# A hybrid RWKV-7 / forgetting-attention layer on one core: all engines' instruction order made with the scheduler's finer timing model

## The chip, the cores and the metric

The kernel runs on one core of one Trainium2 chip. The time is that of the whole launch on the device in microseconds (us). Of several runs the median is taken.

## What is computed

One layer of a streaming encoder is computed for two inputs: 1024 new frames of a prompt (no past) and 64 frames of a running stream (256 cached frames). Cut to what matters:

```python
h    = rms_norm(x, norm1_g) * (1 + sc1) + sh1              # sc, sh, gt: silu(c) @ w_ada + b_ada
proj = h @ w_in                                            # 1792 RWKV columns, 1544 attention columns
z    = p_rwkv + (previous_row(p_rwkv) - p_rwkv) * shift_mu # -> r, k, v, decay, a, g
...
def step(s, inp):                                          # RWKV-7, one frame after the other, 8 heads of 64
    sa = einsum('bhvk,bhk->bhv', s, -kk_t)
    s  = s * w_t + sa * (kk_t * a_t) + v_t * k_t
    return s, einsum('bhvk,bhk->bhv', s, r_t)
...
y_fox = softmax(q k^T / 8 + decay_bias, causal) @ v        # 8 heads of 64, q and k RMS-normed
x = x + gt1 * (concat(y_rwkv, y_fox) @ w_out)
h2 = rms_norm(x, norm2_g) * (1 + sc2) + sh2
x = x + gt2 * ((silu(h2 @ w_ffn_gate) * (h2 @ w_ffn_up)) @ w_ffn_down)
```

Also returned are the last RWKV state and row, and the attention keys, values and log forget values.

## The kernel before

All matrices stand transposed, features on the 128 partitions and frames along the free axis. The frames are cut into two halves: half 0 has prompt frames 0 to 511, half 1 has prompt frames 512 to 1023 and the 64 stream frames (576 columns, handled as two chunks of 288). Every large product is made to near single precision by three matmuls on split operands (`mm3`, L294 to L296: high times high, high times low, low times high, all into one PSUM tile).

The stages, in the order in which the program is written:

- Modulation (L190, L198) and the normed input of half 0.
- For each half a phase (`phase`) that runs a handwritten list of small tasks, `ORDER`: Z are the input projections of one pair of RWKV heads (PSUM tile `pmm`), Q, K, V those of attention, D, A, B and N the RWKV work of one pair of heads, T and U the B and N left over from the half before. There are 4 pairs (j = 0 to 3) in each half, so 8 RWKV chains in all.
- Attention of half 0, attention of half 1 with the output projection of half 0 between its heads, the output projection of half 1.
- The FFN (L1153) in 44 passes of 7 products, and the down projection (L1264).

**One RWKV chain.** The recurrence is done in chunks of 64 frames. A (`rwkv_a`) makes the scaled operands and the chunk matrices (TensorE L464 into `pA`, VectorE L466 into `At`), sends 16x16 blocks through DRAM, solves them with 15 pairs of small VectorE operations (L488, L490) and sends the result back through DRAM. B (`rwkv_b`) joins the blocks with 32x32 matmuls (L523, L549; `pg`, `pw`, `pu`, `pgt`), transposes (`pkbt`, `pvt`), and then walks through the chunks, 8 in half 0 and 9 in half 1, one strictly after the other. One **step** of this walk is:

```python
nc.tensor.matmul(pr, At[:, c, 0], sv[:, c], ...)                    # L597, pR
nc.vector.tensor_copy(R[hsl[0]], pr[hsl[0], 0])                     # L599
nc.scalar.copy(R[hsl[1]], pr[hsl[1], 1])                            # L600
nc.tensor.matmul(py[:, c % 4], sv[:, c], rk[:, c], ...)             # L608, pY
nc.tensor.matmul(pa, inv[:, c], R, ...)                             # L610, pSA
nc.vector.tensor_scalar(sv[hsl[0], c, 0], pa[hsl[0]], -1.0, ...)    # L611
nc.scalar.mul(sv[hsl[1], c, 1], pa[hsl[1]], -1.0)                   # L612
nc.tensor.matmul(pS, kbt[:, c], sv[:, c], ...)                      # L613, pS
nc.vector.scalar_tensor_tensor(d, pS[hsl[h], h], pc[...], sd[...])  # L617, twice; next chunk's sv
nc.tensor.matmul(py[:, c % 4], sv[:, c], At[:, c, 1], ...)          # L618, pY
```

So a step has three **links** in which TensorE needs a result that other engines make of its own last one: pR to pSA (through L599 and L600), pSA to pS (through L611 and L612), pS to the next pR (through L617). GpSimd scales the old state meanwhile (L604, `sd`). The ninth chunk starts from another state, so the link ahead of it is none. N (`rwkv_n`) then normalizes (`bsum`, L375; ScalarE L637, L639; `plora`, L368).

**What sets the order.** The program is written through a tile framework. It records every instruction with its dependences, and when its context closes, a scheduler decides for each of the five engines in which order its instructions stand; tasks written earlier have precedence, and a task that would have to wait lets later ones pass. To judge what would have to wait, the scheduler runs a timing model as it goes. On the chip each engine then takes its instructions in that fixed order, with semaphores between engines. SyncE (SP) issues all DMAs, in its own fixed order. PSUM for the attention of half 1 is only opened when the pools of the RWKV phase are closed. The context is opened in `kernel`:

## Time and profile before

| | |
|---|---|
| median of 3 runs | 1747.09 us (1741.33 to 1749.53) |
| the profiled execution | 1735.94 us |
| its span, first to last instruction | 1734.2 us |
| TensorE matmul busy (PE) | 1663.8 us, 96% |
| TensorE weight load busy (PEld) | 1447.9 us, 83% |
| VectorE busy (DVE) | 1126.6 us, 65% |
| ScalarE busy (ACT) | 729.1 us, 42% |
| GpSimd busy (POOL) | 180.8 us, 10% |

The profile is of one execution. PE and PEld are two rows of one engine: the matmuls, and the loading of the matrices that stay in the array, which runs beside them. PE's ends of matmuls are modelled, so that PE busy is not PE at its peak. A float32 matmul of the program shows as two records. "L597 pR" is line 597 writing tile pR; an arrow in brackets names who ended the idle time before.

### The profile page before, as it was taken

The numbers are of one execution on the slowest core, as the hardware profiler recorded it, in microseconds if no ns is written. First come the engines' busy times: TensorE is split into PE (matmuls) and PEld (weight loads), VectorE is DVE, ScalarE is ACT, GpSimd is POOL, SyncE is SP. The second block draws the span as 40 slices with busy tenths as digits, with TensorE's granted clock in tenths as the row PEclk, the third lists the DMA queues.
The fourth block names the chain that finished last, engine by engine and source line by source line (L and its number), as shares of the span: only waits on it lengthen the run. The fifth ranks groups of instructions, "written<-read, shape, count | busy, mean of one in ns | idle before, by whom it ended". The sixth has DMA issues, their size and how long they took to land.

```text
span 1734.2 us, 33257 instructions
## 1 busy us (share of the span) xinstructions
PE 1663.8 (96%) x12893; PEld 1447.9 (83%) x12893; DVE 1126.6 (65%) x2574; ACT 729.1 (42%) x1532; POOL 180.8 (10%) x412
## 2 busy tenths in 40 slices
PE   5999999999999999889999989999999999999999
PEld 3676766688888888766888889999999999999998
DVE  6676676757686753876877686666666655555545
ACT  4534454553454445765776453333233223211210
POOL 2102121131221212300210000000000000000000
PEclk9999999999899999989999999999999999999999
DMA  8535457632233344566553333222222224433213
GB/s 314 149 95 137 142 140 207 175 93 56 55 76 75 95 121 136 157 194 177 151 177 136 127 115 101 75 75 75 76 75 82 78 87 143 161 98 98 95 37 122
DMA packets 133581, 207.09 MB, mean 119 GB/s; under 512 B 62126, under 2 KB 70350, under 8 KB 133422
## 3 DMA queue, kind: packets, MB, share of 16 engines
q1 hardware_dynamic: 133422, 204.95, 39.3%
q8 instruction: 102, 1.67, 0.4%
q14 instruction: 57, 0.47, 0.1%
HBM read 157.65 MB, written 47.25 MB: 118 GB/s over the span
## 4 chain that ended last, share of the span: by engine, by line
PE 82%; DVE 7%; ACT 7%; DMA 2%; issue 2%; SPq 1%; POOL 0%; DVEq 0%; ACTq 0%; POOLq 0%
PE pd L1264 15%; PE pfc L1153 8%; PE pfe L1153 8%; PE pfa L1153 7%; PE pmm L294 5%; PE pmm L296 5%; PE pmm L295 5%; PE pfb L1153 4%; PE pav L962 2%; PE pbs L375 2%; PE pA L464 2%; PE ppt L940 2%; PE po L294 1%; PE po L295 1%; PE po L296 1%
## 5 line engine op out<-in xcount | busy, mean ns | idle before, releaser
L294 PE MATMUL pmm<-hhi,whi 128*128 128x288 f32 (+1 forms) x624 | 220.7, 354 | 0.7 <-ACT pb L317 0.7
L295 PE MATMUL pmm<-hlo,whi 128*128 128x288 f32 (+1 forms) x624 | 218.2, 350 | 0.0
L296 PE MATMUL pmm<-hhi,wlo 128*128 128x288 f32 (+1 forms) x624 | 218.0, 349 | 0.0
L212 ACT CAST whi<-wraw 128x1024 fp32r<-128x1024 f32 (+2 forms) x116 | 99.3, 856 | 214.4 <-PE pd L1264 167.0
L1264 PE MATMUL pd<-ah,wlo 128*128 128x512 f32 (+1 forms) x528 | 173.5, 329 | 0.0
L1264 PE MATMUL pd<-al,whi 128*128 128x512 f32 (+1 forms) x528 | 173.2, 328 | 0.0
L1264 PE MATMUL pd<-ah,whi 128*128 128x512 f32 (+1 forms) x528 | 173.0, 328 | 0.0
L1268 DVE SCALAR_TENSOR_TENSOR x1t<-pd,mod,x1t 128x512 f32<-128x512 f32 x192 | 91.4, 498 | 110.6 <-PE pd L1264 110.0
L294 PEld LDWEIGHTS pmm<-hhi,whi 128*128 128x128 f32 x624 | 120.3, 193 | 13.5 <-ACT pb L317 2.0
L296 PEld LDWEIGHTS pmm<-hhi,wlo 128*128 128x128 f32 x624 | 120.3, 193 | 10.9 <-issue 1.7
L295 PEld LDWEIGHTS pmm<-hlo,whi 128*128 128x128 f32 x624 | 120.4, 193 | 9.6 <-issue 0.7
L216 DVE TENSOR_TENSOR wlo<-wraw,whi 128x1024 fp32r<-128x1024 f32 (+2 forms) x108 | 103.8, 961 | 26.0 <-ACT whi L212 25.6
L1153 PE MATMUL pfc<-hh,hS 128*128 128x256 f32 (+1 forms) x352 | 102.0, 290 | 4.4 <-ACT hh L1055 4.4
L1264 PEld LDWEIGHTS pd<-al,whi 128*128 128x128 f32 x528 | 99.4, 188 | 7.7
L1264 PEld LDWEIGHTS pd<-ah,whi 128*128 128x128 f32 x528 | 99.3, 188 | 7.7
L1264 PEld LDWEIGHTS pd<-ah,wlo 128*128 128x128 f32 x528 | 99.2, 188 | 7.4
L1153 PE MATMUL pfc<-hl,hS 128*128 128x256 f32 (+1 forms) x352 | 102.3, 290 | 0.0
L1153 PE MATMUL pfc<-hh,lS 128*128 128x256 f32 (+1 forms) x352 | 102.0, 290 | 0.0
L1153 PE MATMUL pfa<-hl,whi 128*128 128x256 f32 (+1 forms) x352 | 101.8, 289 | 0.0
L1153 PE MATMUL pfa<-hh,whi 128*128 128x256 f32 (+1 forms) x352 | 101.7, 289 | 0.0
L1153 PE MATMUL pfa<-hh,wlo 128*128 128x256 f32 (+1 forms) x352 | 101.4, 289 | 0.0
L604 POOL TENSOR_SCALAR sd<-sv,pc 64x64 f32<-64x64 f32 x136 | 72.0, 529 | 172.9 <-DVE sv L617 156.6
(360 smaller groups left out, 4402.0 us busy)
## 6 DMA issues: line engine op xcount, KB each, us to landing
wraw<-in_w_in_dram SPq DMA_DIRECT2D x52, 512.0 KB
wada<-in_w_ada_dram SPq DMA_DIRECT2D x48, 512.0 KB
as<-actscr SPq DMA_DIRECT2D x22, 544.0 KB
wraw<-in_w_gate_dram SPq DMA_DIRECT2D x22, 512.0 KB
wraw<-in_w_up_dram SPq DMA_DIRECT2D x22, 512.0 KB
wraw<-in_w_down_dram SPq DMA_DIRECT2D x40, 256.0 KB
wraw<-in_w_out_dram SPq DMA_DIRECT2D x16, 512.0 KB
actscr<-sg SPq DMA_DIRECT2D x22, 288.0 KB
```

The lines of the kernel that those rows point to most:

```text
L212: nc.scalar.copy(hi, src)
L216: eng.tensor_tensor(lo, src, hi.bitcast(F32), op=ALU.subtract)
L294: nc.tensor.matmul(ps[0:M, 0:n], whi[:, k, 0:M], xhi[:, k, off:off + n], start=(k == 0), stop=False)
L295: nc.tensor.matmul(ps[0:M, 0:n], whi[:, k, 0:M], xlo[:, k, off:off + n], start=False, stop=False)
L296: nc.tensor.matmul(ps[0:M, 0:n], wlo[:, k, 0:M], xhi[:, k, off:off + n], start=False, stop=(k == kt - 1))
L375: nc.tensor.matmul(ps[:, 0:n], w, x[:, off:off + n], start=True, stop=True)
L464: nc.tensor.matmul(pa[h][:, i], kb[hp, c + i], rk[hp, c + i], start=True, stop=True)
L604: nc.gpsimd.tensor_scalar(sd[hsl[h]], sv[hsl[h], c, h], pc[hsl[h], c], None, op0=ALU.mult)
L940: nc.tensor.transpose(pt[0:rows, b - b0, t * P:t * P + qn], p[0:qn, pc:pc + rows], self.ident[0:qn, 0:qn])
L1153: nc.tensor.matmul(ps, l[:, k], r[:, s, k], start=(first and k == 0 and y == 0), stop=(k == 3 and y == 2), skip_group_check=True)
L1264: nc.tensor.matmul(ps[:, 0:n], w[:, i], x[:, t:t + n], start=(i == 0 and y == 0), stop=(i == len(fs) - 1 and y == 2))
L1268: nc.vector.scalar_tensor_tensor(dst, ps[:, so - off:so - off + l], self.mod[:, 40 + o, b:b + 1], dst, op0=ALU.mult, op1=ALU.add)
```

## The change

One argument of the tile context. The instructions, their operands, the pools and the number of buffers remain; the scheduler judges what would have to wait with a finer timing model.

```diff
-    with _tile.TileContext(nc) as tc:
+    with _tile.TileContext(nc, schedule_with_timeline_sim=True) as tc:
```

The order changes on every engine from the start to the FFN; in the down projection it hardly does. Two places on TensorE:

First, the walk of the last of the eight chains (half 1, j = 3; `At_7017` is its chunk matrix), from the eighth of its nine chunks. psc, ppt and pav are products of the attention of half 0. Before:

```order
L597 MATMUL pR_8375<-sv_8213,At_7017 128x128
L608 MATMUL pY_8329<-rk_6998,sv_8213 128x128
L940 MATMUL ppt_8963<-ident_130,p_8893 128x128
L940 MATMUL ppt_8963<-ident_130,p_8904 128x128
L940 MATMUL ppt_8972<-ident_130,p_8893 128x128
L940 MATMUL ppt_8972<-ident_130,p_8904 128x128 x2
L962 MATMUL pav_8984<-ptl_8910,vsx0_8029 128x256
L610 MATMUL pSA_8385<-R_8377,inv1_693 128x64
L962 MATMUL pav_8984<-pth_8909,vsx0_8029 128x256
L962 MATMUL pav_8984<-ptl_8910,vsx0_8029 128x256
L910 MATMUL psc_8992<-k1x1_8032,qsx1_8030 128x512
L912 MATMUL psc_8992<-k2x1_8033,q2x1_8031 128x512
```

The same step with the change, up to the group norm (pbs) that closes the chain:

```order
L597 MATMUL pR_8375<-sv_8213,At_7017 128x128
L608 MATMUL pY_8329<-rk_6998,sv_8213 128x128
L610 MATMUL pSA_8385<-R_8377,inv1_693 128x64
L613 MATMUL pS_8383<-sv_8213,kb_6999 128x128
L618 MATMUL pY_8329<-At_7017,sv_8213 128x128
L597 MATMUL pR_8400<-sv_8213,At_7017 128x128
L610 MATMUL pSA_8411<-R_8402,inv1_693 128x64
L608 MATMUL pY_8409<-rk_6998,sv_8213 128x128
L613 MATMUL pS_8408<-sv_8213,kb_6999 128x128
L618 MATMUL pY_8409<-At_7017,sv_8213 128x128
L375 MATMUL pbs_8613<-y_8242,bmean_635 128x288
L375 MATMUL pbs_8616<-y_8242,bmean_635 128x288
```

The attention products that stood in each link have moved ahead of the walk, and the step's own five matmuls now follow each other.

Second, the place where the last input projection ends (`pmm_8549`, the last V projection; pkv and pkvs are its transposes). Before, it ends inside the walk of the last chain (`sv_8213`):

```order
L294 MATMUL pmm_8549<-hhi_175,whi_8519 128x288
L295 MATMUL pmm_8549<-hlo_176,whi_8519 128x288
L296 MATMUL pmm_8549<-hhi_175,wlo_8520 128x288
L814 MATMUL pkv_8575<-ident_130,fv_8516 128x128 x2
L910 MATMUL psc_8673<-k1x0_8027,qsx0_8025 128x256
L912 MATMUL psc_8673<-k2x0_8028,q2x0_8026 128x256
L916 LDWEIGHTS identb_8663
L916 MATMUL psc_8673<-cmask_8670,identb_8663 128x128
L613 MATMUL pS_8253<-sv_8213,kb_6999 128x128
L618 MATMUL pY_8254<-At_7017,sv_8213 128x128
```

With the change it ends inside the walk of the first chain of half 1 (`At_4747`, `sv_5446`), and the joining of the second chain (`At_5686`) follows:

```order
L295 MATMUL pmm_8549<-hlo_176,whi_8519 128x288
L296 MATMUL pmm_8549<-hhi_175,wlo_8520 128x288
L814 MATMUL pkv_8575<-ident_130,fv_8516 128x128 x2
L613 MATMUL pS_5641<-sv_5446,kb_4729 128x128
L618 MATMUL pY_5642<-At_4747,sv_5446 128x128
L523 MATMUL pg1_6339<-gt_696,At_5686 32x32 x18
L814 MATMUL pkv_8575<-ident_130,fv_8516 128x128 x2
L820 MATMUL pkvs_8583<-ident_130,fv_8516 64x128
L523 MATMUL pw1_6379<-g1_6337,inv1_693 32x32 x9
L523 MATMUL pu1_6401<-inv1_693,g1_6337 32x32 x13
L375 MATMUL pbs_6069<-y_5475,bmean_635 128x288
```

The projections have moved forward against the RWKV chains by nearly three chains: ahead of the last `pmm` row stand 60 of the 68 pR rows before, 41 with the change. Of the 8 groups of pA (L464) none stands behind the last `pmm` row before, two do with the change.

Counted over all eight walks, 192 links lie between one step's matmul and the next that needs its result. In 2 of them no matmul of other work stands before; with the change in 97: by chain 7, 9, 9 and 20 in half 0 and 1, 24, 3 and 24 in half 1. In the links that still hold other work there is more of it than before: in the first walk of half 1 it is 3 to 10 matmuls a link before, and with the change mostly 20 to 29.

## The prediction

> **What bounds the kernel now.** I read the page first, for who is busy and when. The rows are the span, TensorE's two shares and, in 40 slices, the clock that it was granted, in tenths.
>
> ```profile
> span 1734.2 us, 33257 instructions
> PE 1663.8 (96%) x12893; PEld 1447.9 (83%) x12893; DVE 1126.6 (65%) x2574; ACT 729.1 (42%) x1532; POOL 180.8 (10%) x412
> PEclk9999999999899999989999999999999999999999
> ```
>
> TensorE is the bound, and the change takes no work from it, so only waits can come or go. Second I read busy times by stage: the start, the RWKV phases, attention to the end of the output projection, and part of the FFN. Columns are PE, PEld, DVE, ACT, POOL (busy us and count), clock, DMA share and GB/s.
>
> ```profile
> 0.00:40.00 40.00, 22.36 (x287) 13.72 (x288) 25.88 (x73) 18.36 (x38) 8.35 (x36) 0.91 0.87 326
> 40.00:720.00 680.00, 656.16 (x5703) 519.20 (x5702) 460.33 (x1253) 329.86 (x757) 140.64 (x306) 0.98 0.43 118
> 720.00:1040.00 320.00, 294.40 (x1918) 247.21 (x1918) 245.01 (x504) 203.02 (x430) 31.78 (x70) 0.96 0.52 154
> 1040.00:1480.00 440.00, 440.00 (x3478) 438.90 (x3478) 263.38 (x500) 135.63 (x249) 0.00 (x0) 1.00 0.28 91
> ```
>
> From 1040 us on TensorE is full, and no order can gain there. What the change can do it does in the first 1040 us. In the RWKV phases PE lacks only 680 - 656 = 24 us. Third I asked who waits there, and read one step of the recurrence, instruction by instruction. First the waits (total us, times, longest):
>
> ```profile
> PEld pS L613 <- ACT sv L612: 16.2, 47, 1.0
> PEld pSA L610 <- ACT R L600: 12.0, 41, 0.8
> PE pada L190 <- DMA wada<-in_w_ada_dram: 11.5, 2, 11.1
> PE pS L613 <- ACT sv L612: 3.1, 7, 0.8
> PE pSA L610 <- ACT R L600: 0.6, 2, 0.3
> ```
>
> Then the step, in order of time (start, duration, engine, what):
>
> ```profile
> 160.16 0.43 PE L610 MATMUL pSA<-R,inv 128*128 128x64 f32 x2
> 160.40 0.48 PE L294 MATMUL pmm<-hhi,whi 128*128 128x512 f32 x1
> ...
> 160.70 0.22 DVE L611 TENSOR_SCALAR sv<-pSA 64x64 f32<-64x64 f32 x1 [0.84 <-PE pSA L610]
> ...
> 161.01 0.22 ACT L612 ACTIVATE sv<-pSA 64x64 f32<-64x64 f32 x1 [0.91 <-DVE sv L611]
> ...
> 161.28 0.49 PE L613 MATMUL pS<-sv,kb 128*128 128x128 f32 x2
> ...
> 161.61 0.39 PE L618 MATMUL pY<-At,sv 128*128 128x128 f32 x2
> ...
> 161.75 0.48 PE L294 MATMUL pmm<-hhi,whi 128*128 128x512 f32 x1
> 161.81 0.60 DVE L617 SCALAR_TENSOR_TENSOR sv<-pS,pc,sd 64x64 f32<-64x64 f32 x2 [0.89 <-PE pS L613]
> ...
> 162.19 0.97 POOL L604 TENSOR_SCALAR sd<-sv,pc 64x64 f32<-64x64 f32 x2 [1.32 <-DVE sv L617]
> ...
> 162.56 0.46 PE L597 MATMUL pR<-sv,At 128*128 128x128 f32 x2
> ...
> 162.85 0.39 PE L608 MATMUL pY<-rk,sv 128*128 128x128 f32 x2
> ...
> 162.99 0.48 PE L294 MATMUL pmm<-hhi,whi 128*128 128x512 f32 x1
> ...
> 163.05 0.22 DVE L599 COPY R<-pR 64x64 f32<-64x64 f32 x1 [0.64 <-PE pR L597]
> ...
> 163.36 0.21 ACT L600 COPY R<-pR 64x64 f32<-64x64 f32 x1 [2.13 <-DVE R L599]
> ...
> 163.62 0.43 PE L610 MATMUL pSA<-R,inv 128*128 128x64 f32 x2
> ```
>
> From pSA to pSA the step takes 163.62 - 160.16 = 3.46 us: pSA to pS 1.12, pS to pR 1.28, pR to pSA 1.06. Each link is a fixed sequence: matmul, VectorE, ScalarE, matmul (or VectorE twice). The two engines stand idle ahead of their part, so nothing here is queueing. The step's own matmuls hold TensorE for much less, from start to start: pSA 0.24, pS 0.33, pY 0.14, pR 0.29, pY 0.14, together 1.14 us. The other 2.32 us hold projection matmuls. That is why the chains cost so little now: the rows of waits show 28 us of idle weight loading at two kinds of link, and PE itself hardly stops.
>
> **The bare links.** The new order leaves 97 links with no other work before the matmul that waits (front part: 7, 9, 9, 20, 1, 24, 3, 24), against 2. TensorE takes its instructions in order, so a bare link costs its full length less its own matmuls, however far the engine got before, since it starts from TensorE's own last matmul. That is (3.46 - 1.14) / 3 = 0.77 us a link, and 97 x 0.77 = 75 us. Taken off is what such links cost before and no longer do, since every other link now has ample work in it: at most the 16.2 + 12.0 = 28.2 us by weight loads, at least the 3.1 + 0.6 = 3.7 us by PE. The weight load's wait is partly covered by the matmul still running, the PE row sees only what is left of it, so I take the middle, 16. Term: +59 us, between +47 and +71.
>
> **What stands bare beside them.** With the projections gone after the first walk of half 1, the joining of chains 2 to 4 of that half also runs without them, and the norm behind the last chain stands alone, where attention filled both before. The norm, first and last matmul, and one of the copies between:
>
> ```profile
> 728.50 0.65 PE L375 MATMUL pbs<-y,bmean 128*128 128x288 f32 x2
> ...
> 731.49 0.69 ACT L637 ACTIVATE gsq<-y 128x576 f32<-128x576 f32 x1
> ...
> 735.04 0.75 PE L368 MATMUL plora<-z,wg 128*128 128x288 f32 x2 [0.49 <-ACT gsq L639]
> ```
>
> 735.04 - 728.50 = 6.5 us hold four norm matmuls before the plora; by 0.65 to 0.75 us each they fill some 2.8, so 3.7 us open, and about 5 with what follows the last one. A joining has four hops through a copy, and where TensorE met one uncovered it lost:
>
> ```profile
> PE pu L549 <- ACT gt L545: 1.7, 2, 1.5
> ```
>
> 1.7 / 2 = 0.85 us. Three joinings by four hops by 0.85 are 10 us. Term: +15, from 0 (attention still covers them) to +25 (the hops as long as the longest, 1.5 us, with the same norm: 12 x 1.5 + 5 = 23).
>
> **The clock.** Where light stretches of small matmuls came, the granted clock (column after POOL) fell in the next 10 us:
>
> ```profile
> 130.00:140.00 10.00, 9.79 (x228) 6.88 (x227) 5.67 (x15) 4.14 (x11) 0.82 (x2) 1.00 0.38 95
> 140.00:150.00 10.00, 8.36 (x59) 6.14 (x59) 6.81 (x25) 8.31 (x18) 2.25 (x4) 0.66 0.81 234
> 450.00:460.00 10.00, 10.00 (x245) 8.80 (x244) 8.63 (x16) 3.07 (x9) 2.33 (x3) 0.97 0.16 58
> 460.00:470.00 10.00, 10.00 (x64) 8.37 (x64) 5.04 (x10) 2.54 (x6) 4.35 (x7) 0.52 0.18 54
> ```
>
> A fall costs 3.4 to 4.8 us of full speed in such a window. The new order has three long bare walks (20, 24 and 24 links, 1.14 us of matmul in 3.46). If each brings one fall that was not there before, that is 10 to 14 us; inside a walk half speed costs less, as most of it is waiting. I take 7, between 0 and 14. [...]
>
> **What gets better.** Waits in 40 to 720 other than the links: 24 - 4 = 20 us of PE idle. A finer model may place some copies better. I take -6, from 0 to -20. The start keeps its first 11.1 us of DMA wait, as the first loads stand in the same order.
>
> **What is moved at no cost.** The DMA issues of SP change places too (666 rows before, 658 after), among them weight loads. DMA is busy 0.43 in that stage and PE waited for a DMA only at the start, so there is slack; without it a load costs its wait, at most like the first, 11 us. GpSimd's L604 ends at 163.16, two us ahead of the next L617, so it does not lengthen a bare step. FFN and down projection: neighbouring groups change places, DVE and ACT are at 60% and 31% there: 0.
>
> **Sum.** 59 + 15 + 7 - 6 = +75 us on the profiled execution's 1735.94, so about 1811. The runs' median lies 11 us above that execution; I add to the median: 1747 + 75 = 1822. The ends: 47 + 0 + 0 - 20 = +27 (1774) and 71 + 25 + 14 + 0 = +110 (1857).
>
> **Rivals.** *VectorE ends last.* Two of the eight A tasks now stand behind the projections, where attention also needs DVE. Their cost there:
>
> ```profile
> L488 DVE TENSOR_TENSOR tb<-mb,wb x120: 140/200/682, 104.9 to 636.1; 64x15 f32<-64x15 f32 x8, 64x28 f32<-64x28 f32 x8, 64x39 f32<-64x39 f32 x8, 64x48 f32<-64x48 f32 x8
> L439 DVE TENSOR_TENSOR rk<-kk,pp 128x512 f32<-128x512 f32 x2 | 1.4, 683 | 0.0
> ```
>
> Per task 30 small operations of 0.20 us and about 14 like L439 of 0.68: 16 us, twice 32. If copies of the walk queue behind them, links grow longer than 1.15 us, and the time is 1822 + 32 = 1854. For it: DVE is already at 245 of 320 from 720 to 1040. Against it: in the bare walks the new DVE order holds little but the copies. 0.20.
>
> *The early part gains more than the late part loses.* Weight loading idles 680 - 519 = 161 us in the RWKV phases, though PE shows 24. If projections packed without chains between them run as the FFN does, PEld 439 of 440, the part ahead of the last `pmm` shrinks. It decides from about half: 84 us gained make 1738, no change; 100 us make 1722, faster. [...] Against it: much of the 161 is 32x32 and two-record float32 work that no order makes denser, and the long links still alternate with short ones. Faster 0.05, no change 0.05.
>
> That the change does nothing is out: TensorE's order differs in most rows up to the FFN.
>
> **How the numbers follow.** My forecast has 0.70, VectorE 0.20, the gain 0.10 in two halves. The range takes the forecast's ends and VectorE's case with some of its own spread, 1770 to 1875; it leaves out the early gain and little else. A measurement of this kernel tells about 0.5%, 9 us, from no change: faster 0.05, same 0.05, slower 0.90.
>
> **What would show it.** In the new profile: PE busy well below 96%, nearly all of the loss between 150 and about 850 us, and none behind; the waits of PE for ACT sv L612, ACT R L600 and DVE sv L617 at the top of its list, some 60 to 75 us together; three stretches of 24 to 31 us with PE near a third and steps of 3.4 to 3.6 us; a clock below 1.00 beside them. Steps well over 3.5 us with DVE busy mean the VectorE rival. I am wrong if those three waits add up to less than 30 us, or if the stage ahead of the last `pmm` row is shorter than before by more than the walks lose.

## The result, and the profile after

With the change the kernel takes 1981.59 us (median of 4 runs, 1969.76 to 1989.30) against 1744.38 us before (4 runs, 1741.33 to 1749.53) on the same chip: a ratio of 1.1367, 95% interval 1.1329 to 1.1405. It is 237 us slower, where 75 were forecast and 1875 us was the upper end of the range.

The page of the changed kernel first: span, busy times, and the granted clock in 40 slices.

```profile
span 1980.3 us, 33378 instructions
PE 1783.8 (90%) x12893; PEld 1544.9 (78%) x12893; DVE 1142.0 (58%) x2574; ACT 726.5 (37%) x1532; POOL 183.3 (9%) x412
PEclk8999859797779965597599789899999999999999
```

The span is 246 us longer. TensorE runs the same 12893 matmuls, and two things have grown by about as much each: it is busy 1783.8 us instead of 1663.8 (+120), and idle 196.5 us instead of 70.4 (+126). Most of the longer busy time is a slower clock, and the last row shows it: many slices of 5 to 8 tenths, where before there were two 8s and otherwise 9. The mean granted clock is 0.883, against 0.981 before. As the trace records only 0.50 and 1.00, that is some 460 us at half speed, against some 65 before. A smaller part may be that a matmul standing alone reads longer than one in a dense row: pSA lasts 0.43 us, but in the prediction's step the next matmul starts 0.24 us behind it. Next the stages (PE, PEld, DVE, ACT, POOL, clock, DMA share, GB/s): the start, the stretch to the last projection matmul, from there to the end of the last norm, attention with the output projection, and part of the FFN.

```profile
0.00:40.00 40.00, 25.22 (x293) 15.47 (x294) 25.50 (x73) 18.36 (x38) 4.81 (x21) 0.87 0.96 356
40.00:700.00 660.00, 587.72 (x4459) 477.06 (x4459) 367.90 (x942) 270.64 (x575) 108.34 (x243) 0.87 0.37 107
700.00:980.00 280.00, 210.81 (x1472) 155.91 (x1465) 137.82 (x425) 92.48 (x279) 44.45 (x108) 0.62 0.27 75
980.00:1280.00 300.00, 263.18 (x1627) 222.73 (x1626) 206.44 (x377) 168.25 (x328) 25.73 (x40) 0.89 0.39 119
1280.00:1720.00 440.00, 440.00 (x3511) 439.46 (x3510) 268.85 (x507) 132.51 (x251) 0.00 (x0) 1.00 0.28 90
```

The FFN is as full as before. The projections end at 699.0 us, hardly later than before (692.5), although 19 of the 68 pR rows that stood ahead of that point have not run by then (41 instead of 60). The trace shows how the projections are spent: in the first walk of half 1, which has much more other work in its links, a step takes mostly 9 to 11 us, where it took 3.4 to 5.2 before. Then come 280 us in which no projection is left: clock 0.62, TensorE idle for 69 us even so. The last norm ended at 739.7 us before and ends at 978.4 us now, and from there to the FFN it is 236 us (233 before). So the loss lies in the RWKV phases, spread over both halves.

The waits of TensorE (total us, times, longest):

```profile
PE pS L613 <- ACT sv L612: 30.3, 35, 3.2
PE pR L597 <- DVE sv L617: 13.8, 31, 1.8
...
PE pSA L610 <- ACT R L600: 9.7, 27, 1.4
...
PE pbs L375 <- DVE z L451: 6.7, 2, 3.5
...
PE pw L523 <- DVE g L530: 6.1, 4, 3.6
```

The three links hold 53.8 us in these rows, and 58 us with the waits that other engines ended (7 us before). Sorted by whether a link is bare in TensorE's order, some 52 us of it stand in bare links. The links that still hold other work wait some 6 us in all, hardly more than before (5). A bare step of the second walk of half 1, in order of time:

```profile
768.15 0.69 PE L610 MATMUL pSA<-R,inv 128*128 128x64 f32 x2 [0.19 <-ACT R L600]
...
769.53 0.80 PE L613 MATMUL pS<-sv,kb 128*128 128x128 f32 x2 [0.69 <-ACT sv L612]
...
771.11 0.76 PE L597 MATMUL pR<-sv,At 128*128 128x128 f32 x2 [0.36 <-DVE sv L617]
...
772.48 0.69 PE L610 MATMUL pSA<-R,inv 128*128 128x64 f32 x2
```

It takes 772.48 - 768.15 = 4.33 us, not 3.46: pSA lasts 0.69 instead of 0.43 us, pS 0.80 instead of 0.49. Two rows of windows in that walk and one in the joining behind it say why:

```profile
760.00:770.00 10.00, 6.84 (x23) 5.19 (x23) 2.21 (x9) 1.07 (x5) 1.76 (x4) 0.50 0.01 2
770.00:780.00 10.00, 7.37 (x25) 5.52 (x25) 2.99 (x11) 1.22 (x5) 2.21 (x6) 0.50 0.00 0
```

```profile
810.00:820.00 10.00, 9.29 (x73) 7.74 (x73) 4.79 (x10) 0.00 (x0) 0.00 (x0) 0.50 0.08 29
```

The clock stays at 0.50 for the whole walk, though no link in it is idle for more than 0.7 us, and TensorE reads as 93% busy in a joining and still works at half speed.

### The profile page after: what moved, and what is told of

It is laid out like the page before. It is cut to its first block, busy times and chain, and to the rows that moved or that the text cites. A ratio compares the mean times of both kernels' runs of the same rounds, so it can differ in the third digit from the quotient of the medians.

```text
span 1980.3 us, 33378 instructions
## 1 busy us (share of the span) xinstructions
PE 1783.8 (90%) x12893; PEld 1544.9 (78%) x12893; DVE 1142.0 (58%) x2574; ACT 726.5 (37%) x1532; POOL 183.3 (9%) x412
## 4 chain that ended last, share of the span: by engine, by line
PE 73%; DVE 10%; ACT 7%; DMA 6%; issue 3%; SPq 1%; POOL 0%; DVEq 0%; ACTq 0%; POOLq 0%
PE pd L1264 13%; PE pfe L1153 7%; PE pfc L1153 7%; PE pfa L1153 7%; PE pmm L294 5%; PE pmm L295 4%; PE pmm L296 4%; PE pfb L1153 3%; PE pbs L375 3%; PE pav L962 2%; PE pA L464 2%; PE pS L613 1%; PE po L296 1%; PE po L294 1%; PE ppt L940 1%
## 5 line engine op out<-in xcount | busy, mean ns | idle before, releaser
L295 PE MATMUL pmm<-hlo,whi 128*128 128x288 f32 (+1 forms) x624 | 212.4, 341 | 0.0
L296 PE MATMUL pmm<-hhi,wlo 128*128 128x288 f32 (+1 forms) x624 | 212.2, 341 | 0.0
L1153 PE MATMUL pfc<-hh,hS 128*128 128x288 f32 (+1 forms) x352 | 100.9, 287 | 1.3 <-ACT hh L1055 1.3
```

The costliest lines, as they stand in the source:

```text
L295: nc.tensor.matmul(ps[0:M, 0:n], whi[:, k, 0:M], xlo[:, k, off:off + n], start=False, stop=False)
L296: nc.tensor.matmul(ps[0:M, 0:n], wlo[:, k, 0:M], xhi[:, k, off:off + n], start=False, stop=(k == kt - 1))
L1153: nc.tensor.matmul(ps, l[:, k], r[:, s, k], start=(first and k == 0 and y == 0), stop=(k == 3 and y == 2), skip_group_check=True)
```

## The experiments

Three accounts were on the table after the trace. **Theory A**: the projections run out before the chains do, and walks, joinings and norms left without them cost their waits and half the clock besides. **Rival B**: the finer model places the work of the other engines worse as well. **Rival C**: only the bare links count, and the clock has another cause.

### The projections held at the walks (e1_all, e2_half0, e3_half1)

A table gives, for each of the 624 groups of three projection matmuls, the link of the walks that it stood behind in the kernel before; the group may not be issued ahead of it. `links` holds the pR, pSA and pS matmuls as they are traced. In e2_half0 the hold is used for the groups of half 0 alone, in e3_half1 for the others.

```diff
+    def held(self):
+        self.hold += int(HOLD[self.ntri])
+        self.ntri += 1
+        on = self.hold >= 0 and (True)      # e2: self.ntri <= 208, e3: self.ntri > 208
+        return self.tc.issue_after(self.links[self.hold].ins) if on else ExitStack()
...
+        for k in range(kt):
+            with self.held():
+                self.mm3(ps, whi, wlo, xhi, xlo, kt, off, n, M, [k])
```

> The changed kernel, with one thing put back: each group of three projection matmuls may go no earlier, against the links of the walks, than it went in the kernel before; everything else is still placed by the finer model. 21 links are left bare instead of 97, and the walks stand again beside projections. Theory A (walks, joinings and norms left without projections, at half the clock, are the whole loss): the 237 us go but for 21 bare links at about 1 us and as much again beside them, 1760 to 1800 us, granted clock above 0.96. Rival B (the finer model also places copies, loads and VectorE's work worse): the loss stays in the main, above 1900 us. Rival C (only the bare links count, the clock has another cause): about 54 us go, 1925 us, clock still near 0.90.

> The same hold for the projections of the first half alone. Theory A: of the loss the part goes that had come by the end of the projections (82 us at equal work), the stretch behind them stays: 1900 us, from 1880 to 1920. Rival B: 1960 to 1985. Rival C: the bare links of half 0 go from 45 to 18, some 27 us: 1955.

> The same hold for the projections of the second half alone. Here the third chain of half 0 becomes wholly bare (23 links instead of 9), since the projections of half 1 that stood beside it now come later. Theory A: the stretch behind the last projection (154 us lost) comes back, less some 20 us for that chain: 1850 us, from 1825 to 1880. Rival B: 1960 to 1985. Rival C: 52 bare links in all go from half 1 and 14 come in half 0, some 40 us: 1940.

Measured: 1871.98 us (ratio 1.0731, 1.0702 to 1.0760) with both, 1926.66 us (1.1049, 1.1023 to 1.1074) with half 0, 1928.87 us (1.1065, 1.1034 to 1.1096) with half 1. The hold takes back 110 us, 55 and 53 by halves, which add up. No theory is met: theory A alone asked for 1800 at most, rival C for 1925, rival B for over 1900. The page of e1_all:

```profile
span 1871.9 us, 33353 instructions
PE 1712.5 (91%) x12893; PEld 1496.3 (80%) x12893; DVE 1137.3 (61%) x2574; ACT 727.6 (39%) x1532; POOL 201.1 (11%) x412
```

Busy time falls by 71 us of the 120, idle time by only 37 of the 126. So the cover of the walks is worth about 110 us, about two thirds of it by shorter busy time, and 129 us are left with nearly all links covered. The split of the loss into 82 us before the last projection and 154 behind it, from which the two halves were forecast, was no guide to what each half's hold would give.

### Idle work in the bare walks (e4_fill, e7_fill2)

Both add matmuls whose result nobody reads, to the second and fourth walk of half 1, in the order of the changed kernel. In e4_fill they write into the unused part of the tile of the link itself:

```diff
+    def fill(self, ps, ins):
+        with self.tc.issue_after(ins.ins):
+            for _ in range(3):
+                self.nc.tensor.matmul(ps[:, 128:512], self.whi2[0][:, 0:P], self.wlo2[0][:, 0:384], start=True,
+                                      stop=True, skip_group_check=True)
...
+            if hf.smp and j in (1, 3):
+                self.fill(wr, ins)          # behind pR; wa behind pSA, wS behind pS
```

In e7_fill2 they all go into the tile of pS, behind pR's pY and behind pSA, and none stands behind pS.

> The changed kernel, in its own order, with idle work added: behind each of the 51 links of the second and the fourth walk of half 1 stand three matmuls of 128 x 384 whose result nobody reads (153 in all, about 27 us of TensorE's time at full speed). If the clock falls because TensorE is thinly used there (theory A), the fill brings it back: a step goes from 4.33 us to 3.5 to 3.8 in spite of the added work, granted clock near 1.00 in both walks, and the time falls by 10 to 25 us, to about 1960. If the clock there has another cause (rival C), the fill runs at half speed too, 0.35 us each, over 1 us for a link of 0.68 us idle: a step grows to about 5.4 us and the time by about 20 us, to 2000.

> The changed kernel, in its own order, with idle work in the second and fourth walk of half 1, now where it delays no copy: three matmuls of 128 x 384 behind each pR and each pSA, written beside pS, none behind pS (106 or so, about 18 us of TensorE's time at full speed). In the run with fill behind all three the clock rose to 1.00, but each link grew by the fill's own 0.53 us (a step 5.08 us). Theory A: at full clock the fill fits into the gaps of 0.77 us, a step goes from 4.33 us to about 3.5 us, the two walks lose 15 us, and the time is about 1965 us, less than without the added work. Rival C (work added costs its time whatever the clock): a step of 4.33 + 1.05 = 5.4 us and about 2000 us.

e4_fill took 1997.43 us (1.1451, 1.1425 to 1.1477), the time that rival C gave, but not by its way. It holds 162 of these matmuls, 9 more than were announced. Two windows of its second walk:

```profile
780.00:790.00 10.00, 6.73 (x40) 5.39 (x38) 2.42 (x9) 1.22 (x5) 1.76 (x4) 1.00 0.01 2
790.00:800.00 10.00, 6.70 (x39) 5.35 (x38) 2.00 (x8) 0.85 (x4) 2.64 (x6) 1.00 0.00 0
```

The clock is 1.00. A step of e4_fill took 5.08 us (4.33 us without the fill). From the full-speed step of 3.46 us that is (5.08 - 3.46) / 3 = 0.54 us more a link, 0.18 us a matmul: the fill stood in a row with the link, as the copies waited for the fill in their own tile. In the row below the fill (L503) is named as what ended VectorE's wait:

```profile
782.37 0.22 DVE L608 COPY R<-pR 64x64 f32<-64x64 f32 x1 [0.72 <-PE pR L503]
```

In a row with a link, and with twice 0.18 us a matmul at half clock, it would by estimate have been 4.33 + 3 x 1.08 = 7.6 us. e7_fill2, where the copies don't wait, took 1960.94 us (1.1259, 1.1224 to 1.1293), against the changed kernel's 1.1367 with intervals that do not meet. One step of its second walk, and the window around it:

```profile
769.78 0.43 PE L619 MATMUL pSA<-R,inv 128*128 128x64 f32 x2
770.03 0.77 PE L503 MATMUL pS<-wlo,whi 128*128 128x384 f32 x3
770.91 0.49 PE L624 MATMUL pS<-sv,kb 128*128 128x128 f32 x2
771.24 0.39 PE L629 MATMUL pY<-At,sv 128*128 128x128 f32 x2
772.18 0.46 PE L603 MATMUL pR<-sv,At 128*128 128x128 f32 x2 [0.56 <-DVE sv L628]
772.48 0.39 PE L615 MATMUL pY<-rk,sv 128*128 128x128 f32 x2
772.62 0.77 PE L503 MATMUL pS<-wlo,whi 128*128 128x384 f32 x3
773.26 0.43 PE L619 MATMUL pSA<-R,inv 128*128 128x64 f32 x2
```

```profile
770.00:780.00 10.00, 7.99 (x47) 6.26 (x47) 3.43 (x13) 1.48 (x7) 2.66 (x6) 1.00 0.00 1
```

773.26 - 769.78 = 3.48 us, the step that the prediction reckoned with. With 19 us of work added (108 matmuls of 0.18 us) the kernel is 19 us shorter by the ratios. For these two walks it is shown that the clock is low because no other matmuls stand there, and that this costs some 0.85 us a step; rival C falls for them. Whether the clock goes by the time that the matmuls take or by their kind is not shown: the fill is dense 128x384 work of one record a matmul, while the chain's float32 matmuls show as two records each. The walks of half 0, the joinings and the norms were not filled.

### TensorE's whole order (e5_pe_before, e6_pe_finer, e8_meter)

Here the program is traced twice. The first trace is ordered by one model, and the order of chosen engines is read off; in the second each instruction of such an engine is tied behind the one ahead of it, and the other model orders the rest.

```diff
+def hold(tc, orders):
+    ins = {i.name: i for i in tc.nc.cur_bb.bb.instructions}
+    info = mybir.DependencyInfo(mybir.DependencyClass.NoSync, mybir.DependencyReason.DATA)
+    for names in orders:
+        names = [n for n in names if n in ins]
+        for a, b in zip(names, names[1:]):
+            tc.add_manual_dep(ins[b], a, info, reason="order")
...
+    orders += order(build(False, []), [E.PE])
+    nc = build(True, orders)
```

e6_pe_finer has `True` and `False` changed round. e8_meter ties only the projection matmuls, each behind the matmul of the chains (tasks D, A, B, N) that it followed before.

> TensorE's instructions in exactly the order of the kernel before, from the first to the last; VectorE, ScalarE, GpSimd and SyncE as the finer model orders them beside it. With the projections held at the walks alone, 128 us of loss were left. If these too come from TensorE's order (theory A2: what stands bare in the joinings and norms), the time is that of the kernel before, 1735 to 1760 us. If they come from the other engines' order, copies and loads placed worse by the finer model (rival B), it stays above 1830 us.

> The mirror of the one above: TensorE's instructions in exactly the order of the changed kernel, the four other engines as the simple model orders them beside it. Theory A2: the whole loss is there, 1960 to 2000 us. Rival B: the 128 us that the hold at the walks did not bring back are not there, about 1855 us.

> The finer model's order, each projection matmul held behind the one matmul of the chains (walks, joinings, norms) that it followed in the kernel before; the chains among themselves, the other normalisations and attention are free. This meters the projections over the joinings too, not over the walks alone. Theory A2 in its plain form (it is the cover that projections give): 1745 to 1790 us. Rival D (the finer model also orders the chains' own matmuls, the small normalisations and attention worse): it stays between 1800 and 1870 us, near the 1872 of the hold at the walks.

e5_pe_before: 1843.81 us (1.0592, 1.0567 to 1.0617). With every matmul where it was, 103 us are still lost: rival B holds for this part. e8_meter: 1838.81 us (1.0549, 1.0513 to 1.0584), in the range of its rival D, but since the whole order of TensorE gives no more, the rest isn't in TensorE's order at all. So, with the other engines ordered by the finer model, metering the projections over the chains is all that putting TensorE's order back has to give: some 110 us at the walks and some 33 more with the finer metering that takes in joinings and norms (1872 to 1839). e6_pe_finer: 2033.74 us (1.1680, 1.1649 to 1.1712), slower than the change itself and met by neither theory: the finer model's order of the other engines fits its order of TensorE better than the simple model's does. Taken this way round, TensorE's order costs 293 us and the finer model's order of the rest takes 52 us back. The parts of the loss therefore add up only in the order in which they are taken here. The order of the other engines in e5_pe_before is also not that of the changed kernel: the model makes it anew beside TensorE's.

In e5_pe_before the waits of TensorE are for copies, in the same links that were covered before:

```profile
PE pSA L610 <- ACT R L600: 16.2, 17, 2.1
...
PE pS L613 <- ACT sv L612: 11.2, 17, 1.8
```

One of them on VectorE, with the link's own rows on TensorE behind it:

```profile
362.28 0.75 DVE L272 SCALAR_TENSOR_TENSOR hlo<-xk,mod,hhi 128x512 fp32r<-128x512 f32 x1
364.84 0.29 DVE L806 CAST vs<-tok 128x256 fp32r<-128x256 f32 x1 [1.80 <-DMA vscr<-vs]
365.16 0.22 DVE L599 COPY R<-pR 64x64 f32<-64x64 f32 x1
```

```profile
362.39 0.46 PE L597 MATMUL pR<-sv,At 128*128 128x128 f32 x2
...
365.73 0.43 PE L610 MATMUL pSA<-R,inv 128*128 128x64 f32 x2 [1.95 <-ACT R L600]
```

pR is done at 362.85, but L599 stands behind the cast L806, which waits for a store to leave its buffer. The row names ScalarE, as the later of the two copies; what held it was VectorE's queue. The same place in the kernel before:

```profile
326.70 0.22 DVE L599 COPY R<-pR 64x64 f32<-64x64 f32 x1
326.84 0.28 DVE L806 CAST vs<-tok 128x256 fp32r<-128x256 f32 x1
```

There the copy stands ahead of the cast, and pSA starts 1.24 us after pR.

### Which engine's order (e9_pe_act, e10_pe_dve, e11_pe_sp, e12_pe_act_dve)

The same hold, for more engines at a time:

```diff
-    orders += order(build(False, []), [E.PE])
+    orders += order(build(False, []), [E.PE, E.Activation])            # e9
+    orders += order(build(False, []), [E.PE, E.DVE])                   # e10
+    orders += order(build(False, []), [E.PE, E.SP])                    # e11
+    orders += order(build(False, []), [E.PE, E.Activation, E.DVE])     # e12
```

> TensorE's and ScalarE's instructions in the order of the kernel before; VectorE, SyncE and GpSimd by the finer model. With TensorE's order alone 103 us of loss were left, spread over 40 to 1040 us, and TensorE waited there for the copies of the links (ACT R, ACT sv). Theory S: ScalarE, which takes its instructions in order, has work ahead of these copies that cannot start yet (the cast of the next weights, which waits for TensorE to free a buffer, or a square that waits for a load): 1745 to 1780 us. Theory V (the same on VectorE) and theory Q (the DMA issues on SyncE are the cause): 1810 to 1845 us, as with TensorE's order alone.

> TensorE's and VectorE's instructions in the order of the kernel before; ScalarE, SyncE and GpSimd by the finer model. Theory V (VectorE's work queued ahead of the copies): 1745 to 1780 us. Theory S and theory Q: 1810 to 1845 us.

> TensorE's instructions and the DMA issues on SyncE in the order of the kernel before; ScalarE, VectorE and GpSimd by the finer model. Theory Q (a load or store that the finer model issues behind others holds back a copy engine, and that TensorE): 1745 to 1780 us. Theory S and theory V: 1810 to 1845 us.

> TensorE, ScalarE and VectorE in the order of the kernel before; SyncE's DMA issues and GpSimd by the finer model. Theories S and V, one or both: within 0.5% of the kernel before, 1735 to 1750 us. Theory Q: above 1800 us. If it falls between, the queues act on one another, and the shares of the three runs beside it say how.

With ScalarE 1813.98 us (1.0402, 1.0368 to 1.0436), with VectorE 1808.34 us (1.0380, 1.0348 to 1.0412), with SyncE 1853.97 us (1.0634, 1.0601 to 1.0666), with ScalarE and VectorE 1749.30 us (1.0049, 1.0028 to 1.0071). All this is with TensorE's order of before. SyncE's order gives nothing back; theory Q falls. ScalarE's or VectorE's alone gives 30 to 35 us, both together 95. That fits links and hops that go through both engines, so that one queue in a bad order is enough to hold TensorE, but no run shows it by itself. What is left, 8 us, is SyncE's and GpSimd's order together. The page of e12_pe_act_dve stands nearly as the page of before:

```profile
span 1745.8 us, 33280 instructions
PE 1673.1 (96%) x12893; PEld 1455.0 (83%) x12893; DVE 1126.2 (65%) x2574; ACT 729.7 (42%) x1532; POOL 182.8 (10%) x412
```

### What in that order (e13_rest, e14_chain)

TensorE is tied as before; on ScalarE and VectorE e13_rest ties what isn't the chains' own work behind the chains' instruction that it followed, and e14_chain ties the chains' instructions among themselves. `chain` holds what the tasks D, A, B and N trace.

```diff
+    for names in orders[1:]:                                  # e13
+        last = None
+        for n in names:
+            if n in chain:
+                last = n
+            elif last:
+                tc.add_manual_dep(ins[n], last, info, reason="order")
...
+    for names in orders[1:]:                                  # e14
+        names = [n for n in names if n in chain]
+        for a, b in zip(names, names[1:]):
+            tc.add_manual_dep(ins[b], a, info, reason="order")
```

> TensorE in the order of the kernel before; on ScalarE and VectorE all that is not the chains' own work (evacuations and casts of the projections, attention's operands, the loads of x) is held behind the instruction of the chains that it followed before; the chains' own instructions, and SyncE and GpSimd, are placed by the finer model. Theory R: the 95 us that ScalarE's and VectorE's order cost come from such work put ahead of the chains' copies while it cannot start yet: 1745 to 1775 us. Theory K (the chains' own instructions are in a worse order among themselves, say one chain's solve ahead of another's walk): 1815 to 1850 us.

> The mirror: TensorE in the order of the kernel before; on ScalarE and VectorE the chains' instructions are held in their order among themselves of the kernel before, all other work there is placed by the finer model. Theory R: 1815 to 1850 us, hardly better than TensorE's order alone (1844). Theory K: 1745 to 1775 us.

1807.68 us (1.0384, 1.0357 to 1.0410) and 1823.23 us (1.0471, 1.0447 to 1.0494). Neither theory holds by itself: of the 95 us the one gives back 36, the other 21, and neither is enough. The cast ahead of the copy above is a real case of theory R, but not the whole. Which instructions make up the remainder stays open; that it lies in the two queues together is what e12_pe_act_dve shows.

## Why the prediction was wrong

Slower was right, and so was the place: nearly nothing is lost from the FFN on, and the first projection starts no later than before (34 against 35 us). The size was not, 237 us for 75. In the two profiled executions the 246 us of longer span are 51 us of waits at the three links, 75 us of other idle time and 120 us of longer busy time. By the prediction's own steps:

- **The bare links** (+59, 47 to 71): the path was right, since the waits do stand in the bare links, but the near match of the size is partly luck. The 52 us of waits are 0.54 us for each of 97 links, where 0.77 was reckoned, because a part of each bare link reads as busy, the more so at half clock (pSA 0.69 us for 0.43). And all links together had waited some 7 us before, where 16 were taken off. The sign was 60 to 75 us for the three waits; they came to 53.8.
- **The clock** (+7, 0 to 14) is the step that failed most. It was mis-sized: the same matmuls are busy for 120 us more, most of it by the clock. The prediction let the clock fall once in each of three long bare walks and come back after some 10 us. In two of these walks it stayed at 0.50 throughout (a step of 4.33 us), and behind the first of them on through the joining; the mean is 0.62 over 280 us. That inside a walk half speed costs less than double was right (0.87 us a step, where the step's own matmuls of 1.14 us nearly double: from pR to pY 0.56 us for 0.29, from pS to pY 0.59 for 0.33), but pA (444 ns a matmul in the joining from 790 us on, a median of 272 before) and the norms in the joinings ran at half speed too. The falls at 232, 751 and 911 us, with which long half-speed stretches begin, come behind gaps of at most 1.8 us; one at 703 us stands in a gap of 3.6 us.
- **What stands bare beside them** (+15, 0 to 25) failed as well: TensorE's idle time outside the three links grew by some 75 us, the largest item being the waits of the norm matmuls pbs (26 us, before 5). The prediction counted three joinings with four hops each and one norm, all of half 1. Metering the projections more finely, over joinings and norms in both halves (e8_meter against e1_all), is worth 33 us. In half 0, too, whole joinings stand alone, of which the prediction said nothing. Between 225 and 290 us, behind the first walk, not one projection matmul runs, and two windows there read:

```profile
250.00:260.00 10.00, 10.00 (x65) 6.35 (x64) 3.99 (x6) 2.19 (x5) 1.13 (x2) 0.50 0.02 2
...
270.00:280.00 10.00, 6.07 (x46) 4.49 (x46) 7.40 (x25) 4.01 (x11) 2.46 (x5) 0.50 0.13 13
```

  First TensorE is full of the chain's own matmuls at half speed, then it waits for VectorE and ScalarE.
- **What is moved at no cost** spoke of SyncE, GpSimd and the FFN. With the order of the three other engines as before, these are worth 8 us (e12_pe_act_dve). It put no price on the order of ScalarE and VectorE, and that an order of these two can cost much is shown: with TensorE's order of before, it is worth 95 us (e12_pe_act_dve against e5_pe_before). How much of the 237 us it is in the changed kernel stays open. Beside TensorE's changed order the finer model's order of the rest is 52 us better than the simple model's (e6_pe_finer), and in the changed kernel the copies of the links with other work hold TensorE hardly more than before.
- **What gets better** (-6, -20 to 0): no gain shows in the changed kernel, whose idle time outside the links grew.

Of the rivals, *VectorE ends last* did not come as it was put: VectorE's share fell from 65% to 58%. In e5_pe_before it isn't the amount of VectorE's work that holds TensorE, but what its queue puts ahead of a copy. *The early part gains more* did not happen: the stretch up to the last projection is 6.5 us longer with less work in it. Of the signs that were named, the three waits stand at the top of the list, but below the sum that was named. TensorE was to be busy near a third in the bare walks; it reads 68 to 74%, as its matmuls last longer at half clock. The steps of 3.4 to 3.6 us did not come; steps well over 3.5 us were put down to a busy VectorE, which the rows exclude (2.21 of 10 us in the walk).

The loss in the order taken here, from 1981.59 us down to the 1741.63 us of the kernel before in the last of these steps (240 us): 110 by the cover of the walks, 33 by that of joinings and norms, -5 between e8_meter and e5_pe_before (their intervals overlap), 95 by the order of ScalarE and VectorE, 8 by SyncE and GpSimd. The clock is no further item; it is in each of them, as busy time (PE busy 1783.8 us with the change, 1712.5 in e1_all, 1704.7 in e8_meter, 1697.2 in e5_pe_before, 1673.1 in e12_pe_act_dve, 1663.8 before). By either way round TensorE's order is the larger part: 138 us when it is put back first, 293 us when it is put in first.

## What to carry to other kernels

Where TensorE carries short dependent chains beside a stock of dense independent matmuls, the stock has to be metered out so that it lasts as long as the chains; spent early it cost the chains' waits here (52 us in the bare links), and half the clock on much of what ran then (0.62 over 280 us). Count for a new order not only what stands beside a wait on the waiting engine, but what stands ahead of its copies on the engines that serve it: in e5_pe_before one cast that waited 1.80 us for a store on VectorE left TensorE idle for 1.95 us. A lump of loss that is partly longer busy time for the same instructions (here 120 us) is read off the granted clock first (0.883 against 0.981).

## What the runs showed of the hardware

In the bare walks of half 1 the granted clock was low with no gap above 0.7 us within a step. With 1.14 us of matmul (at full speed) in a step of 4.33 us (gaps 0.19, 0.36 and 0.69 us) it was 0.50 throughout; with 1.14 + 9 x 0.18 = 2.76 us in 5.08 us (e4_fill) and 1.14 + 6 x 0.18 = 2.22 us in 3.48 us (e7_fill2, where a gap of 0.56 us a step is left) it was 1.00. So in these walks 26% of TensorE's time, counted at full speed, went with 0.50, and 54% and 64% went with 1.00; the 0.18 us a fill matmul in it is the estimate from the steps above.

The busy share alone does not tell the clock. From 250 to 260 us of the changed kernel TensorE reads as busy all the time and the clock is 0.50, while in e4_fill, from 780 to 790 us, it is 1.00 with TensorE busy for 6.7 of 10 us. In the first window stand 32x32 and float32 matmuls of the chain, in the second also the wide matmuls of the fill. Which property of them counts is not shown.

Idle work that fits into the gaps of two bare chains made the kernel 19 us shorter (e7_fill2, 1.1259 against 1.1367), as much as the work itself lasts (108 x 0.18 us).
